# The last four expert rounds of a routed layer: scatter-add in memory replaced by one-hot matmuls, and the loop for extra rounds moved ahead of the end

## The chip, the cores and the metric

The program runs on one core of one Trainium2 chip. The metric is the device time of one execution in microseconds (us). A core has five engines that run their own instruction streams in order and meet at semaphores: PE (TensorE, matmuls into PSUM), DVE (VectorE), ACT (ScalarE), POOL (GpSimd) and SP (SyncE, which issues transfers here). "PEld" in the profile is PE's weight load. SBUF is the on-chip memory that all engines read, PSUM the one that matmuls write, and the tensors named `...d` (`accd`, `xd`, `modd`, `h2d`) lie in the chip's main memory and are reached by DMA only.

## The reference, cut to what matters

The layer has attention, a long convolution and a mixture of experts; the change touches only what follows the last expert. Each of the 512 tokens `t` (1024 wide) goes to 8 of 64 experts, and what each expert gives is added up with its weight, together with a shared expert:

```python
def step(acc, blk):
    tok, wt, e = blk
    xb = t_pad[tok]
    a = jax.nn.silu(xb @ wg[e]) * (xb @ wu[e])
    out = (a @ wd[e]).astype(jnp.float32) * wt[:, None]
    return acc.at[tok].add(out), None
...
x = x_mixed + mod[:, 5] * moe(h2, ...)
return rmsnorm(x, final_norm)
```

`x_mixed` is the residual stream before the experts; `mod[:, 5]` is one gate value for each of the 1024 channels; the last line divides each token's row by its root mean square and multiplies by `final_norm`.

## The kernel before

Tokens stand as 128 partitions x 4 (`a` = 0 to 3). An expert gets one round of 128 slots: 64 slots for tokens with `a` 0 or 1 and 64 for `a` 2 or 3 (`WIN` = 64). There are 64 static rounds (items `e0` to `e63`), three spare rounds (`s0` to `s2`) for experts whose tokens don't fit in one round, chosen at run time, and a loop (`tc.For_i`, line 1453) for whatever is still left, whose number of turns `nit` is read at run time (line 1452). In the profiled execution it makes no turn.

For a group of up to four rounds `Group.onehot` (DVE, line 1231) makes one-hot matrices from token to slot, and `Group.part` (lines 1250 and 1251) gathers the group's tokens with them on PE. One round is then:

- `wsplit` and `dsplit`: each weight tile, 4 KB for a partition, is split in a high and a low half (`split`, line 105 a cast on ACT, line 106 a subtraction on DVE); a round has six such pairs, four of `gu` and two of `d`;
- `gateup`: 24 matmuls of 512 columns into the PSUM bank `pg`; then a Silu on ACT (line 1055) and a product on DVE (line 1056) give `aa`;
- `apose`: two transposes of `aa` on PE (line 95), split into the pair `aT` by ACT and DVE;
- `down`: 12 matmuls of 512 columns into `py` (two banks, one buffer, tag `y2`);
- `emit`: ACT copies `py` to the SBUF tile `Y` (line 1082; tag `Y`, two buffers), and POOL starts an indirect DMA (line 1083) that adds the 128 rows of `Y` to `accd` at the tokens' places. Each such DMA adds to the same tensor, so each waits for the one before to land.

The raw weights come through a ring of seven tiles of 1 MB (`wr`, `RAW` = 7; three a round, line 995, issued by SP). The pairs of split weights share six buffers (`ws`). The framework's planner sorts the instructions of each engine ahead of time; only those marked `keep_in_program_order` keep their order among themselves.

After the last round and the loop, the end of the kernel (lines 1479 to 1511) loads `final_norm` (`nfn`), the gate (`modE`), the residual (`fx` from `xd`) and the sums (`fa` from `accd`), and for each `a` on DVE multiplies by the gate (L1492), adds the residual (L1493), takes the mean square (on DVE for `a` = 0, L1498, on ACT otherwise, L1500), makes the reciprocal root in seven small steps (L1501 to L1507), scales (L1510) and stores (L1511).

Of the kernel before, what the change touches and what calls it, by code (L numbers as in the profile page):

```python
# [11 lines left out]
F32 = mybir.dt.float32  # L12
# [9 lines left out]
D = 1024  # L22
# [29 lines left out]
def kernel(ctx: ExitStack, tc: tile.TileContext, x, ctxt, wmod, bmod, win, wuq, wuk, wuv, wba, wbh,  # L52
# [929 lines left out]
    def slot_bank(name):  # L982
        return bank(name, 32, "sl").rearrange("p (h e c) -> p h e c", h=2, c=4)
# [3 lines left out]
    class Item:  # L987


        def __init__(self, name, src, xb=None):  # L990
            self.name, self.src, self.xb, self.grp, self.gu, self.parts = name, src, xb, None, [None, None], False

        def wraw(self, name, src):
            t = wp.tile([128, 4, 512], F32, name=name + self.name, tag="wr", bufs=RAW)
            sp.dma_start(t, src)
            return t

# [83 lines left out]
        def emit(self, py, Y):  # L1081
            act.copy(Y, py)  # L1082
            gp.indirect_dma_start(out=accd, out_offset=bass.IndirectOffsetOnAxis(ap=self.ix, axis=0), in_=Y,  # L1083
                                  in_offset=None, compute_op=ALU.add, bounds_check=T - 1, oob_is_err=False)

    def wout_load(n, j):
        return gload(wout[n, :, j], [128, 512], f"wo{n}{j}", pool=opl if j >= 3 else None)
# [128 lines left out]
    def static_src(e):  # L1216
        return lambda: (wgu[e], wd[e])

    class Group:
# [23 lines left out]
        def part(self, k):  # L1243

            name, ni = f"{self.items[0].name}{k}", len(self.items)
            px = bank("px" + name, tag="x1").rearrange("p (i t) -> p i t", i=4)
            js = slice(k * 128, (k + 1) * 128)
            for a in range(NA):
                o, oh = px[:, 0:self.n, win_of(a)], self.oh[:, a]
                pe.matmul(o, h2h[:, a, js], oh, start=(a % 2 == 0), stop=False)  # L1250
                pe.matmul(o, h2l[a][:, js], oh, start=False, stop=(a % 2 == 1))  # L1251
            XT = pair(late, [128, 4, 128], "XT" + name, "XT", XTR)
            split(XT[0][:, 0:ni], XT[1][:, 0:ni], px[:, 0:ni])
            self.XT.append(XT)

# [167 lines left out]
    for e in range(NI + 1):  # L1423
        if e < NI:
            items[e].gateup()
        if e:
            items[e - 1].apose()
        if e == MR:
            more_rounds()
        if e == MR + 4:  # L1430
            for k in range(NS):
                spare_rows.append(dyn_round(spare[k], spos[:, :, k:k + 1], lst[:, 1, k:k + 1], f"s{k}"))
        for q, m in enumerate(cuts[1:-1]):
            for c in {0: range(2, 8), 1: range(2)}.get(m - 1 - e, ()):
                grp[q + 1].part(c)
            if m - 1 - e == 1:
                grp[q + 1].hits(rows(q + 1))
        if e + 1 < NI:
            items[e + 1].wsplit()
        if e:  # L1440
            items[e - 1].down()
        if e in starts and starts[e] + 1 < len(grp):
            grp[starts[e] + 1].onehot()
        if e < NI:
            items[e].dsplit()

        for _ in range(3 if e else 4):
            if loads:
                loads.pop(0)()

    lst2.close()
    n_it = nc.values_load(nit[0:1, 0:1], min_val=0, max_val=62 - NS)
    with tc.For_i(0, n_it, 1) as it:
        e = nc.values_load(elst[0:1, bass.ds(it + NS, 1)], min_val=0, max_val=NE - 1)
        xb = ep.tile([128, D], F32, name="xbov", tag="Y", bufs=2)
        gp.memset(xb, 0.0)
        m = Item("ov", lambda: dyn_src(e), xb)
        for h in range(2):
            m.load_g(h)
        m.load_d()  # L1460
        ps = slot_bank("slov")
        kof = ov.tile([128, 1], F32, name="kof")
        dve.tensor_copy(kof, lst[:, 1, bass.ds(it + NS, 1)])
# [7 lines left out]
        m.ix, m.wg = idx, wgt  # L1471
        m.gather()
        m.xpose()
        m.gateup()
        m.apose()
        m.down()


    with tc.tile_pool(name="fin", bufs=1) as fp:
        nfn = fp.tile([128, D], F32, name="nfn")  # L1480
        sp.dma_start(nfn, nfin.to_broadcast([128, D]))
        modE = fp.tile([128, D], F32, name="modE")
        sp.dma_start(modE, modd[:, 3 * D:].to_broadcast([128, D]))
        ts = [fp.tile([128, D], F32, name=f"fa{a}") for a in range(NA)]
        xs = [fp.tile([128, D], F32, name=f"fx{a}") for a in range(NA)]
        for a in range(NA):
            sp.dma_start(xs[a], xd.rearrange("(p a) d -> p a d", a=NA)[:, a])
        for a in range(NA):
            sp.dma_start(ts[a], accd.rearrange("(p a) d -> p a d", a=NA)[:, a])
        for a in range(NA):  # L1490
            t = ts[a]
            dve.tensor_tensor(t, t, modE, ALU.mult)  # L1492
            dve.tensor_tensor(t, t, xs[a], ALU.add)  # L1493
            ms, sr, rs, nw = (fp.tile([128, 1], F32, name=f"{n}{a}") for n in ("fms", "fsr", "frs", "fnw"))
            sq = fp.tile([128, D], F32, name=f"fs{a}", tag="fs")
            if a == 0:

                dve.scalar_tensor_tensor(sq, t, 1.0 / 1024.0, t, ALU.mult, ALU.mult, accum_out=ms)  # L1498
            else:
                tc.keep_in_program_order(act.activation(sq, t, AF.Square, scale=1.0 / 32.0, accum_out=ms))  # L1500
            dve.tensor_scalar(ms, ms, EPS, None, ALU.add)  # L1501
            tc.keep_in_program_order(act.activation(sr, ms, AF.Sqrt))
            dve.reciprocal(rs, sr)
            dve.tensor_tensor(nw, rs, rs, ALU.mult)
            dve.tensor_tensor(nw, nw, ms, ALU.mult)
            dve.tensor_scalar(nw, nw, -0.5, 1.5, ALU.mult, ALU.add)
            dve.tensor_tensor(rs, rs, nw, ALU.mult)  # L1507
            dst = out.rearrange("(p a) d -> p a d", a=NA)[:, a]
            for cs in (slice(0, D),) if a < 3 else (slice(0, 512), slice(512, D)):
                dve.scalar_tensor_tensor(t[:, cs], t[:, cs], rs, nfn[:, cs], ALU.mult, ALU.mult)  # L1510
                sp.dma_start(dst[:, cs], t[:, cs])  # L1511


# [119 lines left out]
```

## Time and profile before

| | us |
|---|---|
| median of 3 runs | 1361.64 |
| lowest and highest | 1359.26, 1361.69 |
| the profiled execution | 1360.47 |
| its span, first to last instruction | 1358.7 |
| busy: PE, DVE, ACT, POOL | 1282.3, 1059.3, 865.3, 217.1 |

The span is what the trace shows; 1.77 us of the execution lie around it. The page's shares are means over the whole span. The change only touches the last 80 us, so the views are read there: first the busy time by stretch, then the chain that ended last, then the timelines of single engines.

### The profile page before, as it was taken

The numbers are of one execution on the slowest core, as the hardware profiler recorded it, in microseconds if no ns is written. First come the engines' busy times: TensorE is split into PE (matmuls) and PEld (weight loads), VectorE is DVE, ScalarE is ACT, GpSimd is POOL, SyncE is SP. The second block draws the span as 40 slices with busy tenths as digits, with TensorE's granted clock in tenths as the row PEclk, the third lists the DMA queues.
The fourth block names the chain that finished last, engine by engine and source line by source line (L and its number), as shares of the span: only waits on it lengthen the run. The fifth ranks groups of instructions, "written<-read, shape, count | busy, mean of one in ns | idle before, by whom it ended". The sixth has DMA issues, their size and how long they took to land.

```text
span 1358.7 us, 19564 instructions
## 1 busy us (share of the span) xinstructions
PE 1282.3 (94%) x7042; PEld 1053.0 (78%) x7042; DVE 1059.3 (78%) x1631; ACT 865.3 (64%) x1281; POOL 217.1 (16%) x215
## 2 busy tenths in 40 slices
PE   5999999998999999999999999999999999999970
PEld 3687777887777788788888888888888888888750
DVE  3667768995666558768988888988988898888855
ACT  5555553334655246348877787787878888777851
POOL 0000100001242323221111111111111110111120
PEclk9998999998999999999999999999999999999995
DMA  9533566633301465658999998899999999999944
GB/s 328 198 117 127 188 247 226 232 122 110 119 24 55 171 202 180 256 195 295 320 316 321 317 324 289 309 311 322 326 313 324 323 326 324 304 302 304 329 104 173
DMA packets 80903, 328.59 MB, mean 242 GB/s; under 512 B 13508, under 2 KB 15060, under 8 KB 53413
## 3 DMA queue, kind: packets, MB, share of 16 engines
q1 hardware_dynamic: 67300, 301.00, 61.5%
q0 software_dynamic: 11200, 22.14, 8.5%
q10 hardware_dynamic: 2304, 4.20, 0.8%
q8 instruction: 55, 0.90, 0.3%
q14 instruction: 44, 0.35, 0.1%
HBM read 292.71 MB, written 52.97 MB: 254 GB/s over the span
## 4 chain that ended last, share of the span: by engine, by line
PE 59%; DMA 4%; DVE 2%; ACT 1%; issue 1%; DVEq 0%; POOLq 0%; SPq 0%; ACTq 0%
PE pge L92 26%; PE pye L92 13%; PE pxe L1250 5%; PE pxe L1251 4%; PE pout L92 3%; DMA accd<-Ye,ixe 2%; PE pgsh L92 2%; PE pba L92 2%; DMA accd<-Ys,ixs 1%; PE pbh L92 1%; PE pte L95 1%; PE pysh L92 1%; PE sle L92 1%; PE plg L92 0%; DVE fa L1492 0%
## 5 line engine op out<-in xcount | busy, mean ns | idle before, releaser
L1083 POOL DMA_INDIRECT accd<-Ye,ixe x64 | 106.7, 1668 | 606.6 <-ACT Ye L1082 344.2
L1250 PE MATMUL pxe<-oge,h2h 128*128 128x256 f32 x512 | 133.2, 293 | 0.1
L1251 PE MATMUL pxe<-oge,h2l 128*128 128x256 f32 x512 | 128.6, 283 | 0.0
L1251 PEld LDWEIGHTS pxe<-oge,h2l 128*128 128x128 f32 x512 | 97.7, 191 | 3.2
L1250 PEld LDWEIGHTS pxe<-oge,h2h 128*128 128x128 f32 x512 | 97.6, 191 | 3.2 <-issue 0.5
L1082 ACT COPY Ye<-pye 128x1024 f32<-128x1024 f32 x64 | 65.1, 1017 | 6.5 <-PE pye L92 6.0
L790 DVE TENSOR_REDUCE st<-S 128x1 f32<-128x768 f32 x32 | 30.5, 955 | 21.9 <-PE S L92 21.2
L1055 ACT ACTIVATE aae<-pge 128x256 f32<-128x256 f32 x64 | 24.6, 385 | 32.5 <-PE pge L92 32.4
L794 ACT ACTIVATE P<-S,st 128x768 f32<-128x768 f32 x32 | 28.8, 902 | 12.6 <-DVE st L790 10.5
L1231 DVE TENSOR_TENSOR oge<-iot,posm 128x256 fp32r<-128x256 f32 x64 | 23.7, 418 | 13.4 <-PE pxe L1251 13.3
L1056 DVE SCALAR_TENSOR_TENSOR aae<-aae,wge,pge 128x256 f32<-128x256 f32 x64 | 30.5, 476 | 0.5
L811 PE MATMUL pT<-ident,P 128*128 128x128 f32 x192 | 29.7, 276 | 0.0
L92 PE MATMUL po<-PT,V 128*64 128x256 f32 x192 | 29.1, 389 | 0.0
L812 DVE COPY PT<-pT 128x384 f32<-128x384 f32 x32 | 17.6, 549 | 12.5 <-PE pT L811 12.4
L811 PEld LDWEIGHTS pT<-ident,P 128*128 128x128 f32 x192 | 22.1, 140 | 6.2 <-issue 3.1
L92 PEld LDWEIGHTS sle<-R,oge 128*64 128x64 f32 x256 | 23.5, 137 | 4.2
L812 ACT COPY PT<-pT 128x384 f32<-128x384 f32 x32 | 15.2, 476 | 17.1 <-PE pT L811 16.8
L92 PE MATMUL pm<-wm,sc 128*32 128x256 f32 x128 | 14.0, 572 | 11.2 <-DMA wm<-in_wmod_dram 11.1
L95 PE MATMUL pte<-ident,aae 128*128 128x128 f32 x128 | 24.4, 273 | 0.0
L92 PE MATMUL pgsh<-shguh,sx 128*128 128x512 f32 x64 | 23.8, 441 | 0.0
L92 PE MATMUL sle<-R,oge 128*64 128x4 f32 x256 | 23.6, 189 | 0.0
L572 DVE SCALAR_TENSOR_TENSOR u<-raw,vec,u 128x512 f32<-128x512 f32 x24 | 17.9, 748 | 6.7 <-ACT u L570 6.2
(6787 smaller groups left out, 4624.3 us busy)
## 6 DMA issues: line engine op xcount, KB each, us to landing
gu0e<-in_wgu_dram SPq DMA_DIRECT2D x64, 1024.0 KB
gu1e<-in_wgu_dram SPq DMA_DIRECT2D x64, 1024.0 KB
de<-in_wd_dram SPq DMA_DIRECT2D x64, 1024.0 KB
wn<-in_wmod_dram SPq DMA_DIRECT2D x16, 1024.0 KB
wm<-in_wmod_dram SPq DMA_DIRECT2D x16, 512.0 KB
rg<-in_win_dram SPq DMA_DIRECT2D x32, 256.0 KB
rhy<-in_win_dram SPq DMA_DIRECT2D x24, 256.0 KB
specd<-fX POOLq DMA_DIRECT2D x4, 1024.0 KB, 4.8
```

Of the source, the lines that this page charges most:

```text
L92: pin(pe.matmul(o, lhsT, rhs, start=start, stop=stop))
L95: pin(pe.transpose(o, i, idn))
L790: dve.tensor_reduce(st[:, 0:1], S[:, 0:NKEY], AX.X, ALU.max, negate=True)
L794: act.activation(P, S[:, 0:NKEY], AF.Exp, bias=st[:, 0:1], accum_out=rsum[a][:, h % 2:h % 2 + 1])
L811: pe.transpose(pT[:, i * 128:(i + 1) * 128], P[:, kt * 128:(kt + 1) * 128], ident)
L812: (dve.tensor_copy if k3 else act.copy)(PT[:, 3 * k3:3 * k3 + 3, aa * 128:(aa + 1) * 128], pT.rearrange("p (k q) -> p k q", k=3))
L1055: pin(act.activation(self.aa, pg[:, 0:FF], AF.Silu))
L1056: dve.scalar_tensor_tensor(self.aa, self.aa, self.wg, pg[:, FF:], ALU.mult, ALU.mult)
L1082: act.copy(Y, py)
L1083: gp.indirect_dma_start(out=accd, out_offset=bass.IndirectOffsetOnAxis(ap=self.ix, axis=0), in_=Y, in_offset=None, compute_op=ALU.add, bou ...
L1250: pe.matmul(o, h2h[:, a, js], oh, start=(a % 2 == 0), stop=False)
L1251: pe.matmul(o, h2l[a][:, js], oh, start=False, stop=(a % 2 == 1))
```

## The change

The round `e63` and the three spare rounds become `Late` items. Their output no longer goes to `accd`. In `down`, which now goes through the two halves of the columns one after the other, DVE multiplies each half of `py` by the gate, ACT copies it rounded to `Yp[0]`, and DVE subtracts that to get `Yp[1]`. `turn_hits` transposes the round's one-hot matrix (ACT copies it, PE turns it twice, ACT copies the result to `OT`); for `s0` to `s2` it is called at two places of the iteration `e == NE`. After all rounds, `spread` multiplies `OT` (64 slots x 128 tokens) with the two halves of `Yp` into PSUM, for each `a` and each half of the columns, summed over the four rounds; `add_out` adds the two banks to the residual stream. `accd` (now complete after `e62`) and `xd` are loaded in ring tiles while the spare rounds run, and `residual_part` joins them (gate times sum, plus residual) between their outputs. The loop for extra rounds now stands ahead of `spread` and the last norm, and a turn of it adds its output in the same way. `s0` to `s2` keep their `aT` in buffers of their own, and the transposes of `s2` are called in the middle of `down` of `s1`.

```diff
+    class Late(Item):
+        def turn_hits(self, oh):
+            ps = bank("ot" + self.name, 256, "sl")
+            oc = ep.tile([128, D], F32, name="oc" + self.name, tag="Y", bufs=2)
+            oc = oc[:, 0:FF].rearrange("p (k h w) -> p k h w", k=2, h=2)
+            act.copy(oc, oh.rearrange("p (h k) w -> p k h w", h=2).bitcast(F32))
+            for k in range(2):
+                flip(ps[:, k * 128:(k + 1) * 128], oc[:, k].rearrange("p h w -> p (h w)"), ident)
+            self.OT = (ov if self.xb is None else lov).tile([128, 2, 128], FR, name="OT" + self.name)
+            act.copy(self.OT, ps.rearrange("p (k t) -> p k t", k=2))
...
+        def down(self, mid=None):
...
+            for n in range(2):
+                cs = slice(n * 512, (n + 1) * 512)
+                if n and mid:
+                    mid()
...
+                tc.keep_in_program_order(dve.tensor_tensor(Y[:, cs], py[:, cs], lastv(1)[:, cs], ALU.mult))
+                act.copy(self.Yp[0][:, cs], Y[:, cs])
+                tc.keep_in_program_order(
+                    dve.tensor_tensor(self.Yp[1][:, cs], Y[:, cs], self.Yp[0][:, cs].bitcast(F32), ALU.subtract))
+
+        def spread(self, bk, a, n, start, stop):
+
+            hs, cs = slice(a // 2 * WIN, a // 2 * WIN + WIN), slice(n * 512, (n + 1) * 512)
+            for i in range(2):
+                mm(bk, self.OT[hs, a % 2], self.Yp[i][hs, cs], start and i == 0, stop and i == 1)
...
+    items = [(Item if e < NE - 1 else Late)(f"e{e}", static_src(e)) for e in range(NE)]
+    items += [Late(f"s{i}", lambda i=i: dyn_src(spare[i])) for i in range(NS)]
...
+        if k == 2:
+            for i in range(2):
+                accs.extend(halves(ring(f"accs{i}")))
+                for a in (2 * i, 2 * i + 1):
+                    sp.dma_start(accs[a], by_index(accd, a))
...
+    def residual_part(k):
+
+        for a in (range(3), range(3, 5), range(5, 8))[k]:
+            i = (0, 1, 2, 3, 4, 5, 6, 7)[a]
+            tc.keep_in_program_order(
+                dve.tensor_tensor(accs[i], accs[i], lastv(1), ALU.mult) if i < 4 else
+                dve.tensor_tensor(lastv(i - 2), lastv(i - 2), accs[i - 4], ALU.add))
...
+        if e == NE - 6:
+            items[NE - 1].turn_hits(grp[-2].oh[:, :, 3])
+        if e == NE:
+            for i, m in enumerate(items[NE:]):
+                m.turn_hits(grp[-1].oh[:, :, i])
...
+        if e == NE + 1:
+            load_last(2)
+        if e == NI - 1:
+            items[e - 1].down(items[e].apose)
...
+        if e > NE:
+            residual_part(e - NE - 1)
...
+        if e == NE:
+            for i, m in enumerate(items[NE:]):
+                m.turn_hits(grp[-1].oh[:, :, i])
...
+    def out_banks(a, name):
+        if a == 3:
+            t = bank2(f"yo{name}", "y2")
+            return [t[:, 0:512], t[:, 512:]]
+        return [bank(f"yo{name}{a}{n}", 512, t) for n, t in enumerate((("x1", "x1"), ("sl", "pt"), ("pg", "pg"))[a])]
...
     n_it = nc.values_load(nit[0:1, 0:1], min_val=0, max_val=62 - NS)
     with tc.For_i(0, n_it, 1) as it:
...
+    rounds = items[NE - 1:]
+    act.activation(fs[:, 4 * NA:], ones[:, 0:1], AF.Sqrt)
+    for a in range(NA):
+        bks = out_banks(a, "s")
+        for n in range(2):
+            for m in rounds:
+                m.spread(bks[n], a, n, m is rounds[0], m is rounds[-1])
+        add_out(a, bks)
+        last_norm(a, accs[a])
```

## Rows read from the trace of the kernel before

**Rows 1.** Page, first part: busy time, share of span and count by engine.

```profile
PE 1282.3 (94%) x7042; PEld 1053.0 (78%) x7042; DVE 1059.3 (78%) x1631; ACT 865.3 (64%) x1281; POOL 217.1 (16%) x215
```

**Rows 2.** Stretch and length; busy PE, PEld, DVE, ACT, POOL; clock; DMA share; GB/s.

```profile
1280.00:1300.00 20.00, 18.89 (x88) 14.99 (x87) 17.85 (x20) 16.27 (x21) 3.80 (x2) 1.00 0.71 222
1300.00:1310.00 10.00, 10.00 (x45) 8.15 (x44) 7.90 (x9) 7.93 (x10) 3.61 (x2) 1.00 0.22 29
1310.00:1320.00 10.00, 6.68 (x29) 4.64 (x27) 1.48 (x3) 3.41 (x5) 1.72 (x2) 1.00 0.33 54
1320.00:1325.00 5.00, 0.00 (x0) 0.00 (x0) 0.00 (x0) 0.18 (x1) 1.37 (x1) 0.92 0.99 330
1325.00:1330.00 5.00, 0.00 (x0) 0.00 (x0) 0.00 (x0) 0.00 (x0) 1.40 (x1) 0.50 0.78 307
```

**Rows 3.** The chain that ended last: start, us, what.

```profile
1300.66 5.94 DMA accd<-Ye,ixe
...
1328.60 4.48 DMA accd<-Ys,ixs
...
1333.94 3.28 DMA fa<-accd
1337.24 1.24 DVE fa L1492
```

**Rows 4.** Timeline of DVE: start, us, instruction, [idle before <- what ended it].

```profile
1301.67 1.23 DVE L106 TENSOR_TENSOR gs22l<-gu1s,gs22h 128x1024 fp32r<-128x1024 f32 x1 [0.94 <-ACT gs22h L105]
...
1343.06 1.22 DVE L1493 TENSOR_TENSOR fa<-fa,fx 128x1024 f32<-128x1024 f32 x1
1344.19 1.22 DVE L1492 TENSOR_TENSOR fa<-fa,modE 128x1024 f32<-128x1024 f32 x1
...
1353.93 1.41 DVE L1510 SCALAR_TENSOR_TENSOR fa<-fa,frs,nfn 128x512 f32<-128x512 f32 x2
```

**Rows 5.** Timeline of PE: the last two matmuls of `s2`.

```profile
1318.42 0.39 PE L92 MATMUL pys<-dds21l,aTs2h 128*128 128x512 f32 x1
1318.65 0.40 PE L92 MATMUL pys<-dds21h,aTs2l 128*128 128x512 f32 x1
```

**Rows 6.** Groups by shape, 512 wide: busy, mean ns | idle before.

```profile
L105 ACT CAST shguh<-rsg 128x512 fp32r<-128x512 f32 x8 | 5.0, 621 | 5.2 <-DMA rsg<-in_wsgu_dram 5.1
...
L1092 DVE TENSOR_TENSOR to<-pout,modb 128x512 f32<-128x512 f32 x8 | 5.3, 678 | 0.0
...
L106 DVE TENSOR_TENSOR shgul<-rsg,shguh 128x512 fp32r<-128x512 f32 x4 | 2.7, 686 | 3.5 <-ACT shguh L105 3.5
```

**Rows 7.** Timeline of ACT: one `Y` copy, one 256-wide cast, the last Square.

```profile
1299.36 1.02 ACT L1082 COPY Ye<-pye 128x1024 f32<-128x1024 f32 x1
...
1311.11 0.38 ACT L105 CAST aTs1h<-pts 128x256 fp32r<-128x256 f32 x1
...
1350.17 1.04 ACT L1500 ACTIVATE fs<-fa 128x1024 f32<-128x1024 f32 x1
```

**Rows 8.** The loop's line: instructions, ns min/median/max, first and last start.

```profile
L1453 PEldq COMPARE_BRANCH  x3: 92/174/180, 1317.2 to 1334.2; - x3
...
L1453 POOLq INC_SWDGE_SEM  x1: 1335/1335/1335, 1329.4 to 1329.4; - x1
```

**Rows 9.** Busy time by stretch, around an earlier idle time of PE.

```profile
318.40:320.70 2.30, 0.01 (x1) 0.00 (x0) 2.16 (x3) 1.91 (x5) 1.08 (x2) 1.00 0.45 166
...
326.00:327.50 1.50, 1.50 (x5) 1.16 (x4) 1.05 (x2) 0.75 (x2) 0.73 (x1) 0.50 0.38 142
327.50:329.00 1.50, 1.50 (x8) 1.24 (x7) 0.33 (x1) 0.72 (x2) 1.29 (x1) 1.00 0.27 87
```

**Rows 10.** Timeline of PE after that idle time.

```profile
322.47 1.22 PE L92 MATMUL pv<-wuvh,kvnh 128*128 128x512 f32 x2 [4.06 <-ACT wuvh L105]
...
323.91 0.63 PE L92 MATMUL pq<-lq0l,wq0h 128*128 128x512 f32 x1
324.34 0.63 PE L92 MATMUL pq<-lq0h,wq0l 128*128 128x512 f32 x1
```

More of the change, by code (lines that the diff above doesn't have):

```diff
@@ L991, in __init__ @@
             self.name, self.src, self.xb, self.grp, self.gu, self.parts = name, src, xb, None, [None, None], False
+            self.wpool = wp if xb is None else lov
         def wraw(self, name, src):
-            t = wp.tile([128, 4, 512], F32, name=name + self.name, tag="wr", bufs=RAW)
+            t = self.wpool.tile([128, 4, 512], F32, name=name + self.name, tag="wr", bufs=RAW)
             sp.dma_start(t, src)
@@ L1449, with add_out, last_norm @@
                 loads.pop(0)()
-    lst2.close()
+    fin = ctx.enter_context(tc.tile_pool(name="fin", bufs=1))
+    fs = fin.tile([128, NA * 4 + 1], F32, name="fs")
+    ts = [lastv(2 + a) for a in range(NA)]
+    def out_banks(a, name):
[3 more added lines that the diff above has]
+        return [bank(f"yo{name}{a}{n}", 512, t) for n, t in enumerate((("x1", "x1"), ("sl", "pt"), ("pg", "pg"))[a])]
+    def add_out(a, bks):
+        for n, bk in enumerate(bks):
+            cs = slice(n * 512, (n + 1) * 512)
+            dve.tensor_tensor(ts[a][:, cs], ts[a][:, cs], bk, ALU.add)
+    def last_norm(a, o):
+        t = ts[a]
+        ms, sr, rs, nw = (fs[:, 4 * a + i:4 * a + i + 1] for i in range(4))
+        act.activation(o, t, AF.Square, scale=1.0 / 32.0, accum_out=ms)
+        dve.tensor_scalar(ms, ms, EPS, None, ALU.add)
+        act.activation(sr, ms, AF.Sqrt)
+        dve.reciprocal(rs, sr)
+        dve.tensor_tensor(nw, rs, rs, ALU.mult)
+        dve.tensor_tensor(nw, nw, ms, ALU.mult)
+        dve.tensor_scalar(nw, nw, -0.5, 1.5, ALU.mult, ALU.add)
+        dve.tensor_tensor(rs, rs, nw, ALU.mult)
+        for cs in (slice(0, D),) if a < 3 else (slice(0, 512), slice(512, D)):
+            dve.scalar_tensor_tensor(o[:, cs], t[:, cs], rs, lastv(0)[:, cs], ALU.mult, ALU.mult)
+            sp.dma_start(by_index(out, a)[:, cs], o[:, cs])
+    lst3.close()
+    lst4 = ExitStack()
+    lov = lst4.enter_context(tc.tile_pool(name="lov", bufs=1, side="right", reuse_waits="tile"))
+    RAW = 3
     n_it = nc.values_load(nit[0:1, 0:1], min_val=0, max_val=62 - NS)
@@ L1456 @@
         gp.memset(xb, 0.0)
-        m = Item("ov", lambda: dyn_src(e), xb)
+        m = Late("ov", lambda: dyn_src(e), xb)
         for h in range(2):
@@ L1460 @@
         m.load_d()
+        m.Yp = halves(lov.tile([128, 4, 512], FR, name="Ypov"))
         ps = slot_bank("slov")
@@ L1473 @@
         m.xpose()
+        m.turn_hits(oh)
         m.gateup()
@@ L1476 @@
         m.down()
[L1479 to L1485, printed above, removed]
-        for a in range(NA):
[L1487 to L1511, printed above, removed]
@@ new lines @@
+        for a in range(NA):
+            bks = out_banks(a, "ov")
+            for n in range(2):
+                m.spread(bks[n], a, n, True, True)
+            add_out(a, bks)
+    lst4.close()
+    rounds = items[NE - 1:]
+    act.activation(fs[:, 4 * NA:], ones[:, 0:1], AF.Sqrt)
+    for a in range(NA):
+        bks = out_banks(a, "s")
+        for n in range(2):
+            for m in rounds:
+                m.spread(bks[n], a, n, m is rounds[0], m is rounds[-1])
+        add_out(a, bks)
+        last_norm(a, accs[a])
@@ L1515 @@
+    lst2.close()
 _OUT_SHAPE = (1, T, D)
```

56 lines of the change are left out of this document (51 added, 5 removed).

## Prediction, made before the change was run

> **What bounds the kernel now.** The page comes first: PE is busy for 94% of the span and DVE for 78% [rows 1]. That is a mean over stages with different limits, and the change lies in the last one, so the second view is the busy time by stretch [rows 2]. Up to 1310 PE is full (18.89 of 20 us, then 10.00 of 10) with DVE close behind (17.85 of 20, 7.90 of 10); from 1310 to 1320 DVE has almost nothing left (1.48); from 1320 PE and DVE are both at zero. So the last 40 us are bound by something else, and the chain of waits names it [rows 3]: the scatter-adds. That of `e62` lands at 1300.66 + 5.94 = 1306.6, that of `s2` at 1328.60 + 4.48 = 1333.1; four landings in a row thus take 26.5 us, 6.6 each. PE is done with its last `down` long before: its last matmul starts at 1318.65 and lasts 0.40 [rows 5], so T0 = 1319.05. Then come the loop's exit, the load of `accd` (issued 1333.94, used by DVE at 1337.24) and DVE's eighteen microseconds, the last instruction of which starts at 1353.93 and ends at 1355.34 [rows 3, 4]. The span ends at 1358.7, 3.4 us later. From T0 to the end of the span are 39.65 us, and no PE work stands in them.
>
> **What is removed.** Four scatter-adds leave the chain, and with them the wait from T0 to 1333.1. The load of `accd` now waits for the scatter of `e62` only, landing at 1306.6; with the 3.30 us from issue to first use of before [rows 3] the first sums are there near 1310. It leaves the path if DVE reaches them later than that, which it does (below). Eight DVE operations of 1024 columns (four times L1492, four times L1493) leave the end of the kernel; two such start 1.13 us apart (1343.06 and 1344.19 [rows 4]), so 8 x 1.13 = 9.0 us move ahead of the loop. The load of the Sqrt table, nfn, the gate and the residual move forward too; all were hidden behind the scatters, so they count as nothing, and they would cost at most their first-use latency of 3.3 us again if the ring tile that they need came free late. The ring gives seven tiles and the change uses seven after the last weights, each of which needs one weight tile to be split first; the order is that of the rounds, so the gate's tile (needed at `down` of `e63`) waits only for weights of `s1`.
>
> **What is added ahead of the loop.** On DVE each `Late` output costs four operations 512 wide: two products out of PSUM and two subtractions. Alone they take 0.68 and 0.69 [rows 6]; in a row about 0.09 of that overlaps, as with the wide ones (1.22 long, 1.13 apart [rows 4]), so 0.60 each, 2.4 us for a round and 9.6 for four. On ACT two 512-wide copies (0.62 [rows 6]) take the place of one copy of 1.02 [rows 7], and twelve small copies for `turn_hits` of the spare rounds come in (3 rounds x 2 calls x 2; 0.38 each by the 256-wide cast [rows 7]): 4.6 us. ACT has 20 - 16.27 + 10 - 7.93 = 5.8 us of idle time from 1280 to 1310 [rows 2]; I take the cost as nothing, and as 4.6 us at most if none of it falls in the gaps. PE gets fourteen more transposes of 128 columns, under 2 us in all, and saves the waits for `aT` between the last three `down`s; I take that as even. POOL loses four issues; SP has the same loads earlier and in order behind the weights. A wait is added on SP: the four loads of `accd` stand behind the landing of `e62`, and behind them the loads of the residual, which nobody needs before DVE's second part.
>
> **Where DVE comes out.** This is the term that decides. From 1300 on DVE has 7.90 + 1.48 = 9.4 us of old work [rows 2], 9.6 of new outputs and 9.0 of residual work: 28.0 us. It can't start on the new part before 1300, since the first of it needs `down` of `e63`. With no gap it would be through at 1328.0. Gaps there are: the one of 0.94 us on ACT's cast that is there today [rows 4], and, where no old work is left to fill, the wait for ACT's copy between a product and its subtraction. The subtraction of one half is kept ahead of the product of the next, so each half of `s1` and `s2` costs one copy, 0.62 and some hand-over, 0.65 us: four times, 2.6 us. That gives D0 = 1328.0 + 0.9 + 2.6 = 1331.5 for the end of the last residual addition, against T0 = 1319.05 for PE today. PE meanwhile waits: `py` has one buffer, and DVE, not ACT, now empties it. The bounds for D0 are 1328 (all gaps filled) and 1334 (1300 to 1310 keeps all 2.1 us of its idle time and a few casts come late).
>
> **From there to the end.** All engines meet at the loop. Before, the last landing was at 1333.1 and PE's last branch started at 1334.2 and took 0.17 [rows 8], so 1.3 us for the exit when everyone else is there; POOL's step of 1.34 us in it [rows 8] stands ahead of its arrival, I think, and is then hidden; otherwise it adds up to 1.3. With the first weight load I take 2.0, between 1.5 and 3.4. Then 4 values of `a` x 2 halves x 4 rounds x 2 parts = 64 matmuls of 512 columns. At the full clock two start 0.23 us apart (1318.42 and 1318.65 [rows 5]): 14.7 us. But PE has then been idle since about 1324. After T0 today the granted clock is 0.92 over 1320 to 1325 and 0.50 after that [rows 2]; at 318.40 PE had stopped for 4.06 us, came back at 322.47 at 0.50, matmuls 0.43 apart, that is the lower level of 1.2 GHz, and was back at 1.00 from 327.5 on [rows 9, 10]. So 5.0 us at the lower level: 11.6 matmuls, and the other 52.4 x 0.23 = 12.1: 17.1 us. All eight banks are different, so PE doesn't wait for DVE, and DVE's 3.5 us for one `a` (two additions, about 0.9 us of small steps, the scaling) stay under PE's 3.7. After the last matmul: the addition (0.2 + 0.68), from the Square to the last scaling 3.76 (1350.17 to 1353.93 [rows 4, 7]), the scaling 1.41 and the store with what follows 3.4: 9.4 us, between 8.5 and 10.5.
>
> The Trainium skill, "TensorE: Matmul & The Clock Gate", section "What's actually happening", says that the clock gate's default is the throttled state and that activity releases it. Here the trace agrees in kind, at 322.47 and after T0; by that rule the spread costs the 17.1 us above; had the clock stayed full through the wait, it would be 2.4 us less.
>
> **The sum.** 1331.5 + 2.0 + 17.1 + 9.4 = 1360.0 for the end of the span, against 1358.7: +1.3 us. The profiled execution (1360.47) is 1.2 us under the median of the runs, 1361.64; I put the difference on the median: 1362.9. A difference under 0.2% (2.7 us) is about what a measurement of this kernel can't tell from none.
>
> **The rivals.** (1) Faster: DVE isn't the bound. If planner and gaps let it do the first three outputs and both first residual parts by the time PE ends, PE's end stays at 1319.05 and only `s2` follows: a product, a wait, a subtraction (0.2 + 0.6 + 0.65 + 0.6) and three residual additions (3.4): D0 = 1324.5, end 1353.0, -5.7 us: 1355.9. For it speaks that DVE has 8.5 us idle from 1310 to 1320 [rows 2]; against it that the new work ahead of that point is 7.2 + 5.7 us. The bounds of my own sum (1328, 1.5, 17.1, 8.5) reach down to 1355.1 of span, so part of this is between the two.
>
> (2) Slower: the small copies of `turn_hits` stop ACT. Their tiles share the two `Y` buffers, and one is held from the copy at 1299.36 until `e62` lands at 1306.6 [rows 3, 7]. ACT is in order: if such a copy stands ahead of the casts for `s2`'s weights, these wait up to 1306.6 - 1300.4 = 6.2 us, and so do DVE and PE behind them. It decides once the wait is longer than the work DVE has in hand, some 2 to 3 casts. Price up to 6.2: 1369.1.
>
> (3) Slower: the clock doesn't come back, since a matmul here fills 64 rows where those at 322.47 filled 128. Then 64 x 0.43 = 27.5 instead of 17.1: 1373.3.
>
> (4) Faster: matmuls of the two halves of slots overlap. `a` 0 and 1 use rows 0 to 63, `a` 2 and 3 the others; if they ran in pairs, 32 x 0.23 plus 2.5 of clock = 9.9 instead of 17.1: 1355.7. Against it: 32 of one half stand ahead of 32 of the other. The Trainium skill, "TensorEngine Tiling (Array Packing)", section "Key Properties", has tiles operate in parallel; no run here shows a 64-row matmul next to another.
>
> **How the numbers follow.** My forecast 0.38, the faster rivals 0.30 and 0.04, the slower ones 0.20 and 0.08. The forecast's own range is 1358 to 1366 (bounds of D0 and of the loop), with some 0.04 of it under the limit and 0.04 over. That makes faster 0.38, same 0.30, slower 0.32. The range takes in rival 1 and most of rival 2: 1354.5 to 1369.5; outside are rival 3 and the far ends.
>
> **What would show it.** In the profile after: the last residual addition on DVE ends near 1331 with DVE busy for over 9 of 10 us from 1303 on (rival 1: near 1325; rival 2: gaps on ACT casts with ACT waiting for a scatter); the four loads of `accd` are issued near 1306.6 and nobody waits for them; PE's spread starts some 2 us after DVE's last addition, at a granted clock of 0.50 for about 5 us, and takes 17 us; 9.4 us after it the span ends. I am wrong if PE ends its last `down` at 1319 or sooner, if the loop costs over 3.4 us, or if the spread stays at 0.43 us a matmul.

## The result, and the profile after

The changed kernel takes 1374.68 us (median of 4 runs, 1373.40 to 1376.03). The kernel before, run beside it, takes 1360.45 (4 runs, 1358.35 to 1361.69). The ratio is 1.011, with a 95% interval of 1.0097 to 1.0122: about 14 us slower. The forecast was 1362.9, and the upper end of its range 1369.5. One run of e10_adds, below, took 4095.49 us and is left out of its ratio.

The first part of the page, for [rows 1]: busy time, share of the span and count by engine.

```profile
span 1373.9 us, 19760 instructions
...
PE 1311.4 (95%) x7120; PEld 1072.5 (78%) x7120; DVE 1074.2 (78%) x1653; ACT 872.6 (64%) x1302; POOL 209.1 (15%) x211
```

PE has 78 matmuls and 29.1 us of busy time more than in [rows 1]. 64 matmuls at the distance of [rows 5] would have been 14.7 us, so they ran slowly or lie elsewhere. The busy time by stretch, for [rows 2] (stretch and length; busy PE, PEld, DVE, ACT, POOL; granted clock; DMA share; GB/s), tells which:

```profile
1300.00:1310.00 10.00, 8.16 (x38) 5.88 (x37) 7.79 (x10) 6.80 (x16) 0.61 (x1) 1.00 0.59 160
1310.00:1320.00 10.00, 4.92 (x22) 3.17 (x20) 7.01 (x9) 3.12 (x8) 0.00 (x0) 0.97 0.46 182
1320.00:1330.00 10.00, 6.32 (x13) 3.69 (x13) 7.49 (x9) 3.28 (x5) 0.00 (x0) 0.50 0.26 83
1330.00:1340.00 10.00, 3.45 (x8) 2.24 (x9) 5.48 (x6) 1.08 (x2) 0.00 (x0) 0.67 0.06 25
...
1339.35:1365.50 26.15, 26.14 (x64) 19.83 (x64) 10.48 (x27) 5.34 (x10) 0.00 (x0) 0.50 0.15 60
```

Two things are to be seen. The whole spread, 64 matmuls in 26.15 us, runs at a granted clock of 0.50, the lower level of 1.2 GHz. And from 1300 to 1340 neither PE nor DVE is ever full: DVE, which should set the pace, is busy for 7.79, 7.01, 7.49 and 5.48 of 10 us. The chain that ended last (start, us, what), for [rows 3], has no DMA any more:

```profile
1338.48 0.86 issue
1339.35 26.15 PE yos L92 x64
...
1365.52 1.30 DVE last L1582 x2
```

What DVE waits for stands in its timeline, for [rows 4] (start, us, instruction, [idle before <- what ended it]). L1126 is the product out of `py`, L1129 the subtraction, L1374 and L1375 the residual's products and additions:

```profile
1314.29 0.69 DVE L1126 TENSOR_TENSOR Ys<-pys,last 128x512 f32<-128x512 f32 x1 [0.66 <-PE pys L92]
...
1317.41 2.35 DVE L1374 TENSOR_TENSOR accs<-accs,last 128x1024 f32<-128x1024 f32 x2
1319.68 0.68 DVE L1126 TENSOR_TENSOR Ys<-pys,last 128x512 f32<-128x512 f32 x1
1321.05 0.69 DVE L1129 TENSOR_TENSOR Yp66l<-Ys,Yp66h 128x512 fp32r<-128x512 f32 x1 [0.69 <-ACT Yp66h L1127]
1323.38 0.69 DVE L1126 TENSOR_TENSOR Ys<-pys,last 128x512 f32<-128x512 f32 x1 [1.64 <-PE pys L92]
...
1332.83 0.69 DVE L1126 TENSOR_TENSOR Ys<-pys,last 128x512 f32<-128x512 f32 x1 [1.64 <-PE pys L92]
...
1334.82 3.49 DVE L1375 TENSOR_TENSOR last<-last,accs 128x1024 f32<-128x1024 f32 x3
```

The wait of 0.69 for ACT's copy is the one that the forecast counted. The other, 1.64 for PE ahead of a second product, it did not have. The timeline of PE has the other side of it:

```profile
1320.42 0.79 PE L92 MATMUL pys<-dds10h,aTs 128*128 128x512 f32 x1 [3.72 <-DVE Ys L1126]
...
1329.87 0.80 PE L92 MATMUL pys<-dds20h,aTs 128*128 128x512 f32 x1 [2.11 <-DVE Ys L1126]
...
1332.17 0.63 PE L92 MATMUL pys<-dds21h,aTs 128*128 128x512 f32 x1
```

The first matmul of the second half of `s1` starts at 1320.42, just after DVE's product of the first half has ended (1319.68 + 0.68 = 1320.36); PE had stood idle for 3.72 us. The same in `s2`: the product ends at 1329.81, the matmul starts at 1329.87. So the two halves of a `down` go hand over hand, though they lie in two banks: PE's half, then DVE's product, then PE's next half, and only then DVE's next product. In [rows 5] PE was done at 1319.05; here it is at 1332.80.

The forecast's sum against the trace, in the same order:

| step | forecast | measured | off by |
|---|---|---|---|
| last residual addition ends | 1331.5 | 1338.31 | +6.8 |
| from there to the first spread matmul | 2.0 | 1.04 | -1.0 |
| 64 spread matmuls | 17.1 | 26.15 | +9.05 |
| last matmul to end of span | 9.4 | 8.4 | -1.0 |
| end of span | 1360.0 | 1373.9 | +13.9 |

### The profile page after: what moved, and what is told of

Its sections match the earlier page's. It is cut to its first block, busy times and chain, and to the rows that moved or that the text cites. A ratio compares the mean times of both kernels' runs of the same rounds, so it can differ in the third digit from the quotient of the medians.

```text
span 1373.9 us, 19760 instructions
## 1 busy us (share of the span) xinstructions
PE 1311.4 (95%) x7120; PEld 1072.5 (78%) x7120; DVE 1074.2 (78%) x1653; ACT 872.6 (64%) x1302; POOL 209.1 (15%) x211
## 5 line engine op out<-in xcount | busy, mean ns | idle before, releaser
L1084 POOL DMA_INDIRECT accd<-Ye,ixe x63 | 103.3, 1640 | 602.0 <-ACT Ye L1083 376.2
L794 ACT ACTIVATE P<-S,st 128x768 f32<-128x768 f32 x32 | 28.9, 902 | 12.5 <-DVE st L790 10.5
L92 PE MATMUL po<-PT,V 128*64 128x256 f32 x192 | 29.1, 389 | 0.0
L812 ACT COPY PT<-pT 128x384 f32<-128x384 f32 x32 | 15.3, 477 | 17.1 <-PE pT L811 16.8
```

What stands on the lines that cost most here:

```text
L92: pin(pe.matmul(o, lhsT, rhs, start=start, stop=stop))
L794: act.activation(P, S[:, 0:NKEY], AF.Exp, bias=st[:, 0:1], accum_out=rsum[a][:, h % 2:h % 2 + 1])
L812: (dve.tensor_copy if k3 else act.copy)(PT[:, 3 * k3:3 * k3 + 3, aa * 128:(aa + 1) * 128], pT.rearrange("p (k q) -> p k q", k=3))
```

## The experiments

Two theories are to be tested. The clock theory: at the lower level a stream of matmuls that fill 64 rows, one at a time, doesn't bring the clock back. Its rival: what kept the clock low lies ahead of the spread (PE's idle time, 6.55 us before its first matmul), and any stream would have been slow. The tile theory: the second half of a `down` waits for the product of the first because both halves stand in one PSUM tile. Its rivals: the residual's operations on DVE are what takes the time, or the second call of `turn_hits` is.

The table holds four stretches of each profiled execution, read from the timelines of DVE and PE: (a) from the end of the subtraction of `gs20l` (the first weight tile of `s2`) to the end of the last DVE operation ahead of the loop, (b) from there to the first spread matmul, (c) the spread, (d) from its end to the end of the span.

| kernel | a | b | c | d |
|---|---|---|---|---|
| changed kernel | 41.07 | 1.04 | 26.15 | 8.40 |
| e1_rows128 | 54.28 | 1.04 | 17.05 | 8.88 |
| e2_pairs | 41.06 | 1.05 | 9.79 | 15.37 |
| e3_warm | 41.58 | 8.17 | 14.30 | 8.96 |
| e4_splitpy | 34.24 | 1.04 | 26.14 | 8.41 |
| e5_resid | 34.95 | 1.04 | 26.13 | 8.41 |
| e6_oneturn | 39.83 | 1.13 | 26.14 | 8.41 |
| e8_nopairs | 29.50 | 1.04 | 26.14 | 8.42 |
| e7_all | 29.48 | 1.04 | 10.01 | 15.57 |
| e9_pool | 29.85 | 1.04 | 9.36 | 16.21 |
| e11_adds | 29.24 | 1.04 | 9.83 | 17.85 |
| e10_adds | 30.47 | 1.04 | 9.14 | 17.85 |

### e1_rows128: the same matmuls over all 128 rows

`OT` gets a block for each `a` with zeros in the other half of the slots; POOL writes the zeros.

```diff
-            hs, cs = slice(a // 2 * WIN, a // 2 * WIN + WIN), slice(n * 512, (n + 1) * 512)
+            cs = slice(n * 512, (n + 1) * 512)
             for i in range(2):
-                mm(bk, self.OT[hs, a % 2], self.Yp[i][hs, cs], ...)
+                mm(bk, self.OT[:, a], self.Yp[i][:, cs], ...)
```

> Same result, but each spread matmul contracts over all 128 slots: OT gets 128 rows for each a, with zeros in the 64 slots of the other half (written by POOL). Theory A (the granted clock stays at 0.50 through the spread because its matmuls fill only 64 of 128 rows): the spread starts at 0.50 as in the changed kernel, the clock is back at 1.00 some 5 us later as after 322.47 in the kernel before, and the 64 matmuls take 17 us instead of 26.15: 1374.7 - 9 = 1366 us. Theory B (the clock stays down for what came ahead of the spread, the 6.5 us of idle PE and the thin work before that, whatever the matmuls are): 0.50 to the end, 27 us, 1375 us.

1380.49 us (4 runs), ratio to before 1.0147 (1.0130 to 1.0164). The number, the width and the place of the matmuls are those of the changed kernel; only the rows differ. Busy time by stretch over the spread:

```profile
1353.63:1358.00 4.37, 4.37 (x11) 3.45 (x12) 0.55 (x1) 0.00 (x0) 0.00 (x0) 0.52 0.00 0
1358.00:1370.68 12.68, 12.68 (x55) 9.93 (x53) 7.90 (x23) 5.35 (x10) 0.00 (x0) 1.00 0.11 47
```

The clock is back after 4.2 us, and the spread takes 17.05: what the forecast had for it, 17.1. So the idle time ahead of the spread is not what keeps the clock down. The kernel as a whole is slower, where 1366 was expected, since stretch a grew by 13.2 us, and that shows rival 2 of the prediction at work, brought in by the zeros. POOL writes them from 1285.22 on, in one row for 13.48 us, and starts the next scatter only at 1298.98; ACT, which needs the `Y` buffers that the scatters hold, stops three times:

```profile
1285.22 13.48 POOL L1108 TENSOR_SCALAR OTs<-ident 64x128 fp32r<-64x128 f32 x12 [15.65 <-PE pxs L1310]
```

```profile
1304.91 1.01 ACT L1083 COPY Ye<-pye 128x1024 f32<-128x1024 f32 x1 [4.03 <-DMA accd<-Ye,ixe]
...
1311.69 0.41 ACT L1096 COPY ocs<-ogs 128x256 f32<-128x256 f32 x1 [3.87 <-DMA accd<-Ye,ixe]
...
1318.16 0.40 ACT L1096 COPY ocs<-ogs 128x256 f32<-128x256 f32 x1 [3.38 <-DMA accd<-Ye,ixe]
```

### e2_pairs: half-row matmuls, two halves in turn

The matmuls keep their 64 rows; `a` and `a` + 2, which lie in different row halves, alternate.

```diff
+            for i in range(2):
+                for b in (a, a + 2):
+                    hs = slice(b // 2 * WIN, b // 2 * WIN + WIN)
+                    mm(bk[b], self.OT[hs, b % 2], self.Yp[i][hs, cs], ...)
```

> Only the order of the spread is changed: each matmul of a = 0 or 1 (slots 0 to 63) is followed by its twin of a = 2 or 3 (slots 64 to 127). In the changed kernel the last four of a = 1 and the first four of a = 2 started 0.01 to 0.18 us after one another. Theory A: pairs run side by side, 32 x 0.43 = 13.7 us at the lower clock instead of 26.15: 1362 us; if two half-filled matmuls at once count as a full one, the clock also comes back after 5 us: 9.7 us, 1358 us. Rival (matmuls of the two halves run one after the other, the starts at the border being how the profile models ends): 26 to 27 us, 1375 us.

1365.90 us (4 runs), ratio 1.0042 (1.0025 to 1.0059): 8.8 us less than the changed kernel. Its spread takes 9.79 us. Timeline of PE (x2 marks two matmuls that the view puts into one row):

```profile
1345.59 0.63 PE L92 MATMUL yos<-Yp66h,OTs 64*128 64x512 f32 x2
1346.01 0.63 PE L92 MATMUL yos<-Yp66l,OTs 64*128 64x512 f32 x2
...
1348.93 0.40 PE L92 MATMUL yos<-Yp66l,OTs 64*128 64x512 f32 x2
1349.17 0.39 PE L92 MATMUL yos<-Yp67h,OTs 64*128 64x512 f32 x2
```

Two matmuls take the 0.63 us of one and the next two start 0.42 later: they run side by side. And the clock comes back 4.6 us into the spread, as in e1_rows128; the pairs are then 0.23 to 0.24 apart. So its theory held for the spread, with the 9.7 us that it gave for this case; the time missed its 1358 us. Stretch c falls by 16.4 us, but d rises by 7.0: the spread is now so short that most of the norms of all four `a` stand behind it, where three of them stood beside it.

### e3_warm: full-row matmuls ahead of the half-row stream

24 matmuls of 128 rows that nobody reads stand ahead of the spread, which is left as it is.

```diff
+    wk = bank2("warm", "y2")
+    for i in range(24):
+        mm(wk[:, 0:512], h2h[:, 0, 0:128], h2h[:, 1, 0:512])
```

> 24 matmuls with all 128 rows, 512 columns, whose result nobody reads, stand after the loop and ahead of the spread. Both theories: the clock is back at 1.00 some 5 us into them, and they take about 8 us. Theory A (64 rows): the clock falls to 0.50 again while the spread runs without a gap, most of which is at 0.43 us a matmul: 22 to 26 us for the spread, 1374.7 + 8 - 2 = 1380 us. Theory B (what came ahead): the clock stays at 1.00, the spread takes 14.7 us: 1374.7 + 8 - 11.4 = 1371 us.

One run, 1372.87 us. Busy time by stretch:

```profile
1339.00:1343.80 4.80, 3.11 (x7) 2.48 (x8) 0.65 (x1) 0.00 (x0) 0.00 (x0) 0.50 0.00 0
1343.80:1347.81 4.01, 4.01 (x18) 3.00 (x16) 0.00 (x0) 0.00 (x0) 0.00 (x0) 1.00 0.00 0
1347.81:1362.11 14.30, 14.30 (x65) 11.18 (x64) 8.16 (x22) 5.34 (x10) 0.00 (x0) 1.00 0.09 37
```

The clock came up at 1343.80, during the full-row matmuls, and the same 64 half-row matmuls then ran at 1.00 to their end, in 14.30 us. So the stream that doesn't bring the clock back doesn't let it fall either, in these 14.3 us. The time is near theory B's 1371 and not theory A's 1380, while e1_rows128 came out as theory A had it: neither theory holds as it was put, since bringing the clock up and keeping it up differ. The 24 matmuls make stretch b 7.1 us longer (8.17 against 1.04) and eat most of the gain.

### e4_splitpy: a PSUM tile for each half of `py`

```diff
-            py = bank2("py" + self.name, "y2")
             for n in range(2):
                 cs = slice(n * 512, (n + 1) * 512)
+                py = bank(f"py{n}" + self.name, 512, "x1")
```

> The two halves of py in the Late rounds are two PSUM tiles of one bank each (tag x1, free by then) instead of two halves of one tile. Theory: in the changed kernel the matmuls of the second half wait for DVE's product of the first half (they start 0.06 us after its end for e63, s1 and s2) because both lie in one tile. Then here they follow the first half at once, DVE's idle times of 0.66, 1.64 and 1.64 us ahead of the second product vanish, and the last residual addition ends near 1334.4 instead of 1338.3: 1371 us. Rival (the wait is for something else, the buffer of the round before or the planner's order): the second half still starts after the first product, 1374.7 us.

1370.76 us (4 runs), ratio 1.0084 (1.0064 to 1.0103). The two traces stand level ahead of the stretch (the subtraction of `gs20l` starts at 1296.13 here, at 1296.02 in the changed kernel), and a is 6.8 us shorter. DVE's timeline at the place of the rows above:

```profile
1324.16 0.68 DVE L1126 TENSOR_TENSOR Ys<-py0s,last 128x512 f32<-128x512 f32 x1
...
1326.13 0.68 DVE L1126 TENSOR_TENSOR Ys<-py1s,last 128x512 f32<-128x512 f32 x1
1327.50 0.69 DVE L1129 TENSOR_TENSOR Yp67l<-Ys,Yp67h 128x512 fp32r<-128x512 f32 x1 [0.68 <-ACT Yp67h L1127]
1328.11 3.49 DVE L1375 TENSOR_TENSOR last<-last,accs 128x1024 f32<-128x1024 f32 x3
```

The wait for PE ahead of the second product is gone, the wait for ACT's copy is left, and the last addition ends at 1331.6, where the forecast had 1331.5 (and the expectation of this run 1334.4). DVE's busy time over stretch a is nearly that of the changed kernel (29.37 us here, 29.81 there, the rows below under e5_resid), so the gain is idle time: 4.9 us are left of 11.3. The edit takes away two waits at once, since tag `x1` has two buffers: a second half no longer waits for the product of the first, and the next round's first half no longer waits for the product of the second. Both are waits for one tile as a whole; the run doesn't part them. The medians differ by 3.9 us, less than the 6.8 of the traces: the profiled execution of the changed kernel (1375.72) lies 1.0 above its median, that of this kernel (1369.03) 1.7 below.

### e5_resid: the residual's eight operations behind the loop

```diff
-        if e > NE:
-            residual_part(e - NE - 1)
 ...
+        dve.tensor_tensor(accs[a], accs[a], lastv(1), ALU.mult)
+        dve.tensor_tensor(ts[a], ts[a], accs[a], ALU.add)
         add_out(a, bks)
```

> The eight residual operations of DVE (gate times sum, plus residual) stand behind the loop, per a ahead of add_out, instead of between the outputs of the spare rounds. Theory C (DVE and PE take turns ahead of the loop, and every DVE operation there is on the path): the last DVE operation ahead of the loop ends some 9 us earlier than in the changed kernel (1338.3, so near 1329), the eight operations then fit in DVE's idle time of the spread (4.9 + 2.7 us ahead of the first two additions alone), the spread still takes 26 us: 1366 us. Rival (PE's chain of the last rounds sets the end, only the last three additions, 3.5 us, are on the path): 1371 us.

1371.41 us (4 runs), ratio 1.0083 (1.0050 to 1.0115): the rival's 1371 us, not theory C's 1366. The planner still put the four products ahead of the loop, in DVE's gaps; the four additions came behind it, beside the spread, and cost nothing there (d is the same). Stretch a is 6.1 us shorter, though `py` is one tile. Busy time over stretch a tells how much of that is work (the changed kernel, e5_resid, and e4_splitpy):

```profile
1297.25:1338.31 41.06, 24.91 (x87) 16.64 (x87) 29.81 (x36) 17.04 (x31) 1.55 (x1) 0.81 0.33 110
```

```profile
1296.83:1331.77 34.94, 23.09 (x87) 15.08 (x87) 25.17 (x32) 16.98 (x31) 1.94 (x1) 0.95 0.41 133
```

```profile
1297.36:1331.60 34.24, 21.29 (x82) 14.69 (x80) 29.37 (x36) 16.77 (x33) 1.55 (x1) 0.86 0.40 132
```

Of the 6.1 us, 4.6 are DVE's work that left the stretch (29.81 against 25.17), the four additions. Its idle time fell by only 1.5, from 11.3 to 9.8 us. So the residual's operations cost what they last, and are not what makes the gaps: without the additions PE and DVE still take turns. How long DVE waits at such a turn goes with PE's clock, as DVE's timeline shows:

```profile
1318.58 0.69 DVE L1126 TENSOR_TENSOR Ys<-pys,last 128x512 f32<-128x512 f32 x1 [1.29 <-PE pys L92]
...
1327.25 0.69 DVE L1126 TENSOR_TENSOR Ys<-pys,last 128x512 f32<-128x512 f32 x1 [0.23 <-PE pys L92]
...
1329.70 0.69 DVE L1126 TENSOR_TENSOR Ys<-pys,last 128x512 f32<-128x512 f32 x1 [0.38 <-PE pys L92]
```

The wait of 1.29 stands behind six matmuls at 0.50, those of 0.23 and 0.38 behind matmuls at 1.00 (PE's timeline at the first of the six, and busy time by stretch):

```profile
1315.61 0.80 PE L92 MATMUL pys<-dds00h,aTs 128*128 128x512 f32 x1 [1.85 <-DVE Ys L1126]
```

```profile
1315.60:1318.50 2.90, 2.89 (x6) 1.83 (x6) 1.69 (x2) 0.61 (x1) 0.00 (x0) 0.50 0.28 114
```

```profile
1320.00:1332.00 12.00, 6.48 (x23) 3.52 (x21) 8.36 (x11) 4.31 (x6) 0.00 (x0) 1.00 0.25 89
```

At the full clock six matmuls (6 x 0.23) fit nearly beside ACT's copy and DVE's subtraction; at 0.50 (6 x 0.43) they don't. In the changed kernel two residual products (1317.41, 2.35 us) stand on DVE ahead of the product at 1319.68, PE waits 3.72 us, and from 1320.42 on its matmuls are at 0.50. That these products are what brings the lower clock is argued, not shown: in e5_resid the clock fell as well, behind a wait of 1.85 us, but was back at 1.00 for the rounds after.

### e6_oneturn: `turn_hits` once for each spare round

```diff
-        if e == NE:
-            for i, m in enumerate(items[NE:]):
-                m.turn_hits(grp[-1].oh[:, :, i])
```

(the second of the two places)

> The second of the two places where the one-hot matrices of s0 to s2 are transposed is left out (six ACT copies, 2.3 us, six transposes on PE, 0.8 us). Theory C (DVE sets the pace): 1374 us, no change that can be told. Rival 2 of the prediction (ACT's small copies hold up its casts): 3 us or more less, 1371 us.

1375.39 us (4 runs), ratio 1.0104 (1.0068 to 1.0139). The interval takes in the changed kernel's 1.011, so no cost of the doubled transposes and copies can be told. It is wide, though: it reaches some 5 us to either side, and the prediction's upper bound for the copies was 4.6. Stretch a is 1.2 us shorter. Taking them as nothing is not contradicted.

### e8_nopairs and e7_all: the repairs together, without and with pairs

e8_nopairs joins e4_splitpy, e5_resid and e6_oneturn; e7_all adds the order of e2_pairs.

> e7_all without the pairs: two PSUM tiles for the halves, the residual behind the loop, one call of turn_hits, but the 64 half-row matmuls in the order of the changed kernel. Theory (the half-row stream doesn't raise the clock, and pairs do): the spread takes 26 us at 0.50, the start of it is near 1330 as in e7_all, the time some 8 to 10 us over e7_all: 1366 to 1368. Rival (it was the length of PE's idle time ahead of the spread that kept the clock low in the changed kernel, and this kernel's PE stands idle for less): the clock is back after some 5 us, the spread takes 17 us, the time is about 1360.

> Four edits together: paired order of the spread, py in two tiles, residual behind the loop, one transpose of the one-hot matrices. If their gains add: the last DVE operation ahead of the loop near 1322, the spread 7.4 to 9.8 us (at once at 1.00 if PE has been idle too short for the clock to fall), and then DVE sets the end: 9.1 us of residual, 4.8 of additions, 8.6 of norms from about 1323.5, 3.4 us for the store: span 1350, 1352 us, 9 us less than the kernel before. If the clock or the planner's order eats it: 1358 us or more.

e8_nopairs: 1365.64 us (5 runs), ratio 1.0049 (1.0032 to 1.0066). e7_all: 1357.55 us (10 runs), ratio 0.9984 (0.9968 to 1.0000). The two differ in the order of the 64 matmuls, and with it in that of the additions and norms behind them. Busy time by stretch over the spread of each, e8_nopairs first:

```profile
1327.98:1354.13 26.15, 26.14 (x64) 19.83 (x64) 15.01 (x31) 5.34 (x10) 0.00 (x0) 0.50 0.15 60
```

```profile
1329.90:1335.00 5.10, 5.10 (x24) 4.01 (x26) 4.29 (x4) 0.00 (x0) 0.00 (x0) 0.50 0.00 0
1335.00:1339.91 4.91, 4.91 (x42) 3.65 (x40) 3.04 (x7) 2.72 (x5) 0.00 (x0) 1.00 0.00 0
```

PE's idle time ahead of the spread is nearly the same in both (4.27 and 4.61 us), and shorter than the 6.55 of the changed kernel; still the single half-rows stay at 0.50 for 26 us and the pairs don't. Pairs gain 16.1 us in c and give back 7.2 in d; the medians differ by 8.1. That is e8_nopairs' theory, and its rival (1360) fell. e7_all missed its 1352: the last DVE operation ahead of the loop ended at 1328.17 and not near 1322, and d is 15.57 us.

### e9_pool, e10_adds, e11_adds: what holds the end then

e9_pool is e7_all with the residual's four products on POOL, between the spare rounds. e10_adds and e11_adds are e9_pool and e7_all with all additions of the spread's banks ahead of all norms.

```diff
+            for a in ((0, 1), (2,), (3,))[e - NE - 1]:
+                gp.tensor_tensor(accs[a], accs[a], lastv(1), ALU.mult)
```

```diff
         for b in bks:
             add_out(b, bks[b])
-            last_norm(b, accs[b])
+    for b in (0, 2, 1, 3):
+        last_norm(b, accs[b])
```

> As e7_all, but the four products of gate and sum are made by POOL between the spare rounds (2.4 us each by its 1024-wide subtractions, 9.6 us in all, from about 1309), the additions stay on DVE behind the loop. If POOL's work is free: 4.5 us of DVE work less behind the loop than in e7_all, 1348 us. If POOL and DVE slow one another, or the loop waits for POOL: 1352 us or more.

> e9_pool with one order changed: all four pairs of additions of the spread's banks to the residual stand on DVE ahead of the four norms, instead of the norms of a = 0 and 2 standing ahead of the additions of a = 1 and 3. In e9_pool the spread ended at 1335.3 and the additions of a = 1 and 3 came only at 1340.5, the span ended at 1351.5, 16.2 us after the last matmul. Theory (the order on DVE holds the end): additions right behind the last matmul (4 x 0.6 = 2.4 us), then the norms of four a with Square on ACT about 1.2 each: last Square some 7 us after the last matmul, the last scaling and store 4 more, so 11 to 13 us from the last matmul to the end: 3 to 5 us less than e9_pool, about 1353 us, 0.4% faster than before. Rival (four norms of some 3 us on DVE and ACT fill the end whatever the order): 16 us stay, 1357 us.

> e7_all with the same order as e10_adds: all additions ahead of the norms. Theory: 3 to 5 us less than e7_all, about 1353.5. Rival: no change, 1357.5.

e9_pool: 1356.81 us (10 runs), ratio 0.9984 (0.9967 to 1.0000). e10_adds: 1359.64 (12 runs), ratio 0.9991 (0.9978 to 1.0004). e11_adds: 1358.13 (11 runs), ratio 0.9994 (0.9982 to 1.0005).

Four products less on DVE, 4.5 us, should have shortened stretch a of e9_pool, and it is 29.85 against 29.48. DVE's busy time in it even rose, from 24.52 us (e7_all, first row) to 25.36 (e9_pool):

```profile
1299.38:1328.86 29.48, 20.05 (x76) 13.99 (x74) 24.52 (x32) 14.94 (x27) 1.55 (x1) 0.87 0.47 153
```

```profile
1295.05:1324.90 29.85, 20.17 (x76) 13.77 (x74) 25.36 (x28) 14.92 (x27) 12.25 (x5) 0.85 0.46 151
```

The timelines of POOL and DVE in e9_pool tell where the gain went:

```profile
1305.65 10.70 POOL L1563 TENSOR_TENSOR accs<-accs,last 128x1024 f32<-128x1024 f32 x4 [7.76 <-DMA accs<-accd]
```

```profile
1306.84 1.74 DVE L1129 TENSOR_TENSOR Yp<-Ye,Yp 128x512 fp32r<-128x512 f32 x1
1308.51 2.84 DVE L1129 TENSOR_TENSOR Yp<-Ys,Yp 128x512 fp32r<-128x512 f32 x1
1311.27 0.68 DVE L1126 TENSOR_TENSOR Ys<-py1s,last 128x512 f32<-128x512 f32 x1
...
1312.64 1.49 DVE L1129 TENSOR_TENSOR Yp<-Ys,Yp 128x512 fp32r<-128x512 f32 x1
...
1315.14 1.76 DVE L1129 TENSOR_TENSOR Yp66l<-Ys,Yp66h 128x512 fp32r<-128x512 f32 x1
```

While POOL's products run, four subtractions of DVE take 1.74, 2.84, 1.49 and 1.76 us in place of 0.68: 5.1 us more, against the 4.5 that were moved. The products out of PSUM keep their 0.68. In e10_adds, which has the same products on POOL, the four take 2.12, 2.83, 1.49 and 1.54. So e9_pool missed its 1348 us, and no difference to e7_all can be told. The Trainium skill, "GPSIMD Engine Reference", section "1. Specifications", says that GpSimd shares its SBUF interfaces with VectorE and that DVE instructions with two SBUF inputs contend with it; the trace agrees: the subtraction, which reads both inputs from SBUF, is stretched, and the product, one of whose inputs is in PSUM, is not.

The order of the end was a miss: d grew to 17.85 us instead of falling to 11 to 13. In e10_adds each Sqrt on ACT now waits for DVE to be through with the norm before it:

```profile
1349.79 0.20 ACT L1595 ACTIVATE fs<-fs 128x1 f32<-128x1 f32 x1 [2.39 <-DVE fs L1594]
1352.38 0.20 ACT L1595 ACTIVATE fs<-fs 128x1 f32<-128x1 f32 x1 [2.38 <-DVE fs L1594]
```

Four norms in a row at 2.59 us each are 10.4 us of the 17.85: the rival, that four norms fill the end whatever the order, fits better. It isn't parted from another cause: my order may have had a share, since I had also pinned the first step of each norm on DVE, and the steps of two norms no longer mixed as they do in e7_all.

## Why the prediction was wrong, point by point

- **What bounds it, and the removal:** right. No scatter is on the chain after. The four loads of `accd` are issued at 1305.12 (forecast 1306.6), and nobody waits for them.
- **DVE's work from 1300:** right. 28.0 us forecast; 27.8 measured (7.79 + 7.01 + 7.49 and 5.48 in the rows by stretch). Its sign failed all the same: DVE was to be busy for over 9 of 10 us from 1303 on, and was so for 5.48 to 7.79. The work was counted rightly, but DVE alone did not set the pace. Rival 1, that PE's end would stay at 1319.05, fell: PE's last `down` ended at 1332.80.
- **The gaps on DVE: wrong, +6.8 us.** The step was the 0.9 + 2.6 = 3.5 us of gaps in "D0 = 1328.0 + 0.9 + 2.6 = 1331.5". They were 10.5 (38.3 less 27.8). By DVE's timeline 3.9 of them are three waits for PE ahead of a second product (0.66, 1.64, 1.64), which the forecast had at nothing; 4.5 are waits for ACT's copy, six and not four, one of them 1.03; 1.4 is the cast, forecast at 0.9; the rest are small. The prediction did say that "`py` has one buffer, and DVE, not ACT, now empties it", and charged this to PE alone. What failed is "each half of `s1` and `s2` costs one copy": it looked at one half's product and subtraction, and took the second half's matmuls as done beside them. They wait for the product of the first half, and at 0.50 it is 3.0 us from the end of that product (1329.81) to the start of the next (1332.83). e4_splitpy takes the wait away and ends at 1331.6 in its profiled execution, near the forecast's number; by the medians that edit is worth 3.9 us. e5_resid shows that the wait is small (0.38) while PE's clock is at 1.00, and 1.29 at 0.50.
- **The loop:** 1.04 against 2.0, below my lower bound of 1.5. All engines but DVE were there long before, and POOL's step of [rows 8] doesn't show on the path.
- **The spread: wrong, +9.05 us.** The step was "5.0 us at the lower level", read from [rows 9, 10], where the matmuls filled 128 rows. Rival 3 named just this and had 0.08; its 27.5 us stand against 26.15 measured (the four pairs at the border from `a` = 1 to 2 save most of the difference). The rows said nothing on 64-row matmuls, so the case in which the lower level stays should have had far more than 0.08. Activity alone did not bring the clock back here: 64 matmuls back to back ran at 0.50 to their end. e1_rows128 changes the rows alone and gets the 17.05 us of the forecast; e2_pairs and e3_warm show that half rows are not slow as such.
- **The last part:** 8.4 against 9.4, just under its lower bound of 8.5. This term and the loop came out 2.0 us too long together and hide as much of the two misses.
- **Rival 2:** not in this kernel (ACT waited 0.36 us for a scatter in all), but no fantasy: in e1_rows128 it stops ACT for 4.03 + 3.87 + 3.38 us.
- **Rival 4:** the overlap is real. The Trainium skill, "TensorEngine Tiling (Array Packing)", section "Key Properties", has different tiles run in parallel, and e2_pairs agrees: two matmuls in the 0.63 us of one. In the changed kernel the order of the loops keeps them apart but for four pairs, at the border from `a` = 1 to 2.
- **From span to median:** I put the profiled execution 1.2 us under the median; that of the changed kernel lies 1.0 over it.

What stays open: why the clock fell ahead of the second half of `s1` in the changed kernel and stayed down, and in e5_resid came back, is not shown. By what the chip judges a stream of matmuls is not shown; the runs show that single 64-row matmuls left the clock at 0.50 for 26 us in five kernels (the changed one, e4_splitpy, e5_resid, e6_oneturn, e8_nopairs), and that 128 rows or pairs raised it. And the gain of e7_all over the kernel before, 0.2%, has an interval that ends at 1.

## What to carry over

When a stage with matmuls is put behind an idle stretch of PE, price it at the lower clock unless the trace shows that matmuls of just this shape bring the clock back, and alternate row halves where there are two. When the engine that empties a PSUM tile changes, write down for each half who waits for whom: two banks in one tile are one thing to wait for. And a stage that becomes short uncovers the work that ran beside it (here 7 of 16 us), so look at what it hid before counting the gain.

## What the hardware showed that I had not expected

- Half-row matmuls one at a time left the granted clock at 0.50 for 26.15 us, yet held it at 1.00 for 14.30 us once it was up (e3_warm).
- Two 64-row matmuls of 512 columns in different row halves took the time of one: a pair each 0.43 us at the lower level and 0.23 at the full one.
- POOL's products of two SBUF tensors stretched DVE's 512-wide subtractions from 0.68 to as much as 2.84 us (e9_pool; 2.83 in e10_adds), and left its products out of PSUM at 0.68.
